# Storing the last tile of a rotary embedding in two pieces of four rows

## Chip, cores and metric

One core of a Trainium2 chip. The metric is the device time of one execution in microseconds (us).

In the text and the profiles, PE is the matmul engine (TensorE), DVE is VectorE, ACT ScalarE, POOL GpSimd, SPq the sync engine's queue, which issues the transfers, and L83 is line 83 of the kernel. A transfer has landed when its last bytes are written. Each transfer here is carried by 16 DMA engines in packets; the packet records give each packet's start, duration and size, but not its engine, so packets were chained end to start to follow one engine.

## The reference

```python
batch, seq, dim, num_heads = 16, 512, 1024, 16       # head_dim 64, half 32, float32
x = x.reshape(batch, seq, num_heads, head_dim)
x1, x2 = x[..., :half], x[..., half:]
out = concatenate([x1*cos - x2*sin, x1*sin + x2*cos], axis=-1)
```

32 MiB come in, 32 MiB go out, and each element gets two products and a sum.

## The kernel before

The batch is worked in 8 tiles of 128 partitions x 8192 floats: a partition holds 8 rows ("rows" 0 to 7) of 1024 floats, so a tile is 4 MiB and one partition's share a contiguous 32 KB in HBM. Five tiles fit on chip (three buffers of 1, 2 and 2 tiles), and each is worked in place. All loads and stores but one small table go out from the sync engine's queue, in program order.

```python
def store(t):
    nc.sync.dma_start(out=out_v[t], in_=tiles[t])
def store_two(t):
    nc.sync.dma_start(out=out_v[t : t + 2].rearrange("t p f -> p t f"), in_=both(t))
...
def stores(t):
    if t == 4:
        store_two(3)
    elif t != 3:
        store(t)
    if t == 2:
        load(5)
        load_two(6)
...
for t in range(NT):                              # NT = 8
    ...                                          # row 0: DVE, PE, then ACT copies it back
    pair_sum(*p1, b1)                            # rows 1, 2 on DVE
    ...
    pair_sum(*p2, b2)                            # rows 4, 5 on DVE
    pe_half(ROW_PE, *h1)                         # row 3: second half, ACT copies it back
    p1 = pair_product(t, third[0])
    ...
    pair_sum(*p1, b1)                            # rows 6, 7: the tile's last DVE instruction
    stores(t)
```

GpSimd makes the sine products (but for row 0, where DVE does), DVE the cosine products and most sums. Rows 0 and 3 are summed on PE and copied back by ACT.

Of the kernel before, what the change touches and what calls it, by code (L numbers as in the profile page):

```python
# [26 lines left out]
def kernel(  # L27
# [13 lines left out]
    nc = tc.nc  # L41
    P = nc.NUM_PARTITIONS
    batch, seq, dim = x.shape
# [4 lines left out]
    KK = seq // PB  # L48
    NT = batch // NB
# [3 lines left out]
    out_v = out.rearrange("(t b) (p k) h d -> t (b p) (k h d)", b=NB, k=KK)  # L53
# [14 lines left out]
    tiles = [places[t % len(places)] for t in range(NT)]  # L68
    first_of = [sum(HOMES[:i]) for i in range(len(HOMES))]

    def both(t):

        return homes[first_of.index(t % len(places))]

    def load(t, lo=0, hi=KK):
        s = slice(lo * dim, hi * dim)
        nc.sync.dma_start(out=tiles[t][:, s], in_=x_v[t][:, s])

    def load_two(t):
        nc.sync.dma_start(out=both(t), in_=x_v[t : t + 2].rearrange("t p f -> p t f"))  # L80

    def store(t):
        nc.sync.dma_start(out=out_v[t], in_=tiles[t])  # L83

    def store_two(t):
        nc.sync.dma_start(out=out_v[t : t + 2].rearrange("t p f -> p t f"), in_=both(t))
# [21 lines left out]
    for ps in (own_ps[:, :BANK], own_ps[:, BANK:], pe_ps):  # L108
# [9 lines left out]
        out=spread.rearrange("p (b q) -> p b q", b=NB),  # L118
        in_=bass.AP(tensor=eye.tensor, offset=eye.offset, ap=[eye.ap[0], [0, NB], [1, PB]]),
# [79 lines left out]
    def stores(t):  # L199
        if t == 4:  # L200
            store_two(3)
        elif t != 3:
            store(t)
        if t == 2:
            load(5)
            load_two(6)

    cos_product(own_ps, rows(0, ROW_OWN), ROW_OWN)
    for t in range(NT):
        first, second, third = PAIRS  # L210
        b1 = sin_rows(t, first[0], 2)
        p1 = pair_product(t, first[0])
        r0 = rows(t, ROW_OWN)
        own_product(r0)
        for ps, r in zip(parts(own_ps), parts(r0)):
            pe_add(ps, swapped(r))
        nc.scalar.copy(out=r0, in_=own_ps)  # L217
        b3 = sin_rows(t, ROW_PE, 1)
        b2 = sin_rows(t, second[0], 2)
        pair_sum(*p1, b1)  # L220
        h0, h1 = zip(parts(rows(t, ROW_PE)), parts(b3))
        pe_half(ROW_PE, *h0)
        p2 = pair_product(t, second[0])
        b1 = sin_rows(t, third[0], 2)
        pair_sum(*p2, b2)
        pe_half(ROW_PE, *h1)
        p1 = pair_product(t, third[0])
        if t + 1 < NT:
            cos_product(own_ps, rows(t + 1, ROW_OWN), ROW_OWN)
        pair_sum(*p1, b1)  # L230
        stores(t)
# [35 lines left out]
```

## Time and profile before

| | before |
|---|---|
| median of the first 3 runs | 162.31 us (162.19 to 162.6) |
| span of the profiled execution | 160.6 us |
| DVE, GpSimd, PE, ACT busy | 85%, 79%, 35%, 11% |
| main DMA queue, share of 16 engines' span | 97.8% |
| bytes moved, mean rate over the span | 67.25 MB, 419 GB/s |

The span runs from the first instruction to the last; the time also has what lies around it, about 1.7 us. "16 engines" are those that move the data of every transfer.

### The profile page before, as it was taken

The page shows a single profiled execution, that of the slowest core. Times are in us where ns is not written, and L with a number is a line of the kernel's source. Part 1 is how long each engine was busy: PE and PEld are TensorE (multiplying, and loading weights), DVE is VectorE, ACT ScalarE, POOL GpSimd, SP SyncE. Part 2 cuts the span into 40 slices and gives each one's busy share as a digit, 9 for nine tenths or more (in the row PEclk, how much of TensorE's full clock was granted, in tenths as well). Part 3 has the DMA queues.
Part 4 walks back from the last instruction along what each step waited for, and adds up shares of the span by engine and source line. Part 5 has one row for each costly group of instructions (what it writes and reads, how often), then busy time and mean ns, then how long its engine had stood idle before and what let it go on. Part 6 is the DMA issues. An engine that isn't in the chain of part 4 may idle for free.

```text
span 160.6 us, 431 instructions
## 1 busy us (share of the span) xinstructions
PE 56.2 (35%) x71; PEld 18.8 (12%) x71; DVE 136.4 (85%) x85; ACT 18.1 (11%) x25; POOL 127.1 (79%) x38
## 2 busy tenths in 40 slices
PE   3043905073505550282209140835055502822000
PEld 0021201030102110121003000301021101210000
DVE  1079979999999999999999999999999999998000
ACT  0003301003100301030101210031003010301000
POOL 1059999999999999988998799982999999960000
PEclk9999985559555855576556855595558555765555
DMA  5999999999999999999999999999999999999993
GB/s 187 401 408 473 392 490 424 392 433 482 392 392 522 392 392 522 392 392 498 410 400 465 441 400 408 498 392 408 498 400 400 506 400 400 473 433 400 433 465 147
DMA packets 2561, 67.25 MB, mean 419 GB/s; under 512 B 256, under 2 KB 384, under 8 KB 384
## 3 DMA queue, kind: packets, MB, share of 16 engines
q1 hardware_dynamic: 2480, 67.18, 97.8%
q10 hardware_dynamic: 80, 0.07, 0.1%
q14 instruction: 1, 0.01, 0.0%
HBM read 33.69 MB, written 33.55 MB: 419 GB/s over the span
## 4 chain that ended last, share of the span: by engine, by line
DVE 43%; DMA 34%; issue 7%; POOL 7%; PE 1%; DVEq 0%; SPq 0%
DVE x L197 21%; DVE pd L149 18%; DMA x<-in_x_dram 18%; DMA out_dram<-x 12%; POOL b L173 7%; DMA b<-in_sin_dram 4%; DVE pe_ps L149 2%; PE pd L121 1%; DVE sns L124 0%; DVE sns L125 0%; DVE own_ps L149 0%; DVE x L158 0%; DVEq L197 0%; SPq L80 0%; SPq L83 0%
## 5 line engine op out<-in xcount | busy, mean ns | idle before, releaser
L173 POOL TENSOR_TENSOR b<-x,sns 128x2048 f32<-128x2048 f32 (+1 forms) x32 | 126.4, 3989 | 15.4 <-DVE sns L125 8.6
L197 DVE TENSOR_TENSOR x<-pd,b 128x2048 f32<-128x2048 f32 x24 | 54.9, 2287 | 2.3 <-POOL b L173 1.5
L149 DVE TENSOR_TENSOR pd<-x,tab 128x2048 f32<-128x2048 f32 x24 | 55.0, 2292 | 0.2
L184 PE MATMUL own_ps<-x,ident 128*128 128x512 f32 x32 | 28.9, 1059 | 53.6 <-DVE x L158 48.6
L184 PE MATMUL pe_ps<-b,ident 128*128 128x512 f32 x32 | 25.2, 880 | 29.2 <-DVE pe_ps L149 29.2
L184 PEld LDWEIGHTS own_ps<-x,ident 128*128 128x128 f32 x32 | 9.4, 324 | 73.6 <-DVE x L158 59.6
L217 ACT COPY x<-own_ps 128x1024 f32<-128x1024 f32 x8 | 8.1, 1012 | 72.3 <-PE own_ps L184 72.3
L189 ACT COPY x<-pe_ps 128x512 f32<-128x512 f32 x16 | 9.4, 588 | 40.8 <-PE pe_ps L184 40.8
L184 PEld LDWEIGHTS pe_ps<-b,ident 128*128 128x128 f32 x32 | 8.0, 280 | 43.7 <-DVE pe_ps L149 36.1
L149 DVE TENSOR_TENSOR pe_ps<-x,tab 128x512 f32<-128x512 f32 x16 | 11.0, 686 | 0.0
L149 DVE TENSOR_TENSOR own_ps<-x,tab 128x1024 f32<-128x1024 f32 x8 | 9.8, 1224 | 0.3 <-DMA x<-in_x_dram 0.2
L158 DVE TENSOR_TENSOR x<-x,tab 128x1024 f32<-128x1024 f32 x8 | 9.7, 1214 | 0.0
L124 DVE TENSOR_SCALAR sns<-pd 128x256 f32<-128x256 f32 x1 | 0.4, 425 | 7.5 <-PE pd L121 7.5
L121 PE MATMUL pd<-b,spread 64*128 64x256 f32 x2 | 1.2, 697 | 5.2 <-DMA b<-in_sin_dram 5.2
L217 ACT ACT_TABLE_LOAD x1 | 1.3, 1283 | 14.8 <-DVE x L158 14.8
L109 PE MATMUL own_ps<-zero 128*128 128x512 bf16 x2 | 1.0, 621 | 1.2 <-DVE zero L105 1.2
L121 PEld LDWEIGHTS pd<-b,spread 64*128 64x128 f32 x2 | 0.5, 310 | 6.1 <-issue 6.1
L122 PE MATMUL tab<-b,spread 64*128 64x256 f32 x2 | 1.1, 631 | 0.0
L105 DVE MEMSET zero<- 128x256 uint32 x1 | 0.3, 272 | 0.9 <-PEq L248 0.9
L122 PEld LDWEIGHTS tab<-b,spread 64*128 64x128 f32 x2 | 0.7, 334 | 0.2
L109 PE MATMUL pe_ps<-zero 128*128 128x512 bf16 x1 | 0.6, 634 | 0.0
L109 PEld LDWEIGHTS <-zero 128*128 128x128 bf16 x3 | 0.3, 124 | 1.5 <-DVE zero L105 1.2
(9 smaller groups left out, 1.8 us busy)
## 6 DMA issues: line engine op xcount, KB each, us to landing
out_dram<-x SPq DMA_DIRECT2D x6, 4096.0 KB, 21.9
x<-in_x_dram SPq DMA_DIRECT2D x2, 8192.0 KB, 39.1
x<-in_x_dram SPq DMA_DIRECT2D x3, 4096.0 KB, 27.7
out_dram<-x SPq DMA_DIRECT2D x1, 8192.0 KB, 33.1
x<-in_x_dram SPq DMA_DIRECT2D x1, 2560.0 KB, 12.0
x<-in_x_dram SPq DMA_DIRECT2D x1, 1536.0 KB, 6.8
b<-in_sin_dram ACTq DMA_DIRECT2D x1, 64.0 KB, 7.0
b<-in_cos_dram SPq DMA_DIRECT2D x1, 64.0 KB, 6.7
```

Of the source, the lines that this page charges most:

```text
L105: nc.vector.memset(zero, 0.0)
L109: nc.tensor.matmul(out=ps, lhsT=zero[:, :P], rhs=zero, start=True, stop=True)
L121: nc.tensor.matmul(out=sin_t, lhsT=spread, rhs=sin_sb, start=True, stop=True)
L122: nc.tensor.matmul(out=cos_t, lhsT=spread, rhs=cos_sb, start=True, stop=True)
L124: nc.vector.tensor_scalar_mul(out=sns[:, :, 0, :], in0=sin_k, scalar1=-1.0)
L149: nc.vector.tensor_tensor(out=o, in0=i, in1=cb, op=ALU.mult)
L158: nc.vector.tensor_tensor(out=heads(r), in0=heads(r), in1=s, op=ALU.mult)
L173: nc.gpsimd.tensor_tensor(out=o, in0=i, in1=sb, op=ALU.mult)
L184: nc.tensor.matmul(out=ps, lhsT=ident, rhs=other, start=False, stop=True, skip_group_check=True)
L189: nc.scalar.copy(out=r, in_=pe_ps)
L197: nc.vector.tensor_tensor(out=r, in0=ps, in1=b, op=ALU.add)
L217: nc.scalar.copy(out=r0, in_=own_ps)
```

## The change

It means to shorten the tail: rows 0 to 3 of the last tile are finished before rows 6 and 7, so their half of the store can be issued before the last DVE sum.

```diff
-    def store(t):
-        nc.sync.dma_start(out=out_v[t], in_=tiles[t])
+    def store(t, lo=0, hi=KK):
+        s = slice(lo * dim, hi * dim)
+        nc.sync.dma_start(out=out_v[t][:, s], in_=tiles[t][:, s])
...
         if t == 4:
             store_two(3)
+        elif t == NT - 1:
+            store(t, 0, KK // 2)
+            store(t, KK // 2)
         elif t != 3:
             store(t)
```

## The prediction

> **What bounds the kernel now.** I started with the page's busy totals, its slices and its table of DMA queues, because they disagree about the bound. DVE is busy 85% of the span and the chain that ended last gives DVE 43%, but the DMA queues show hardly any slack:
>
> ```profile
> PE 56.2 (35%) x71; PEld 18.8 (12%) x71; DVE 136.4 (85%) x85; ACT 18.1 (11%) x25; POOL 127.1 (79%) x38
> ...
> DVE  1079979999999999999999999999999999998000
> ...
> DMA  5999999999999999999999999999999999999993
> ...
> q1 hardware_dynamic: 2480, 67.18, 97.8%
> ...
> DVE 43%; DMA 34%; issue 7%; POOL 7%; PE 1%; DVEq 0%; SPq 0%
> ```
>
> The packets of queue q1 take 97.8% of 16 engines' span of 160.6 us, that is 157.0 us on each engine. The DMA row stands at 9 in every slice but the first and the last, while DVE has nothing to do in the last three slices (some 12 us). A DMA share of 34% in the chain means only that the chain is followed back through DVE where a store waited for a sum; it doesn't mean that the queue was ever empty. So the end is set by bytes: 67.18 MB through 16 engines. Outside those 157.0 us lie about 1.7 us until the first data moves, about 1.2 us after the last packet, and some 0.6 us of anything else.
>
> Then I looked at the end, which is all that the change touches. The timeline of the last instructions, and the DMA queue's own waits from 100 us on:
>
> ```profile
> 145.46 0.59 ACT L189 COPY x<-pe_ps 128x512 f32<-128x512 f32 x1 [4.92 <-PE pe_ps L184]
> 145.60 2.29 DVE L197 TENSOR_TENSOR x<-pd,b 128x2048 f32<-128x2048 f32 x1
> ...
> 147.96 0.33 SPq L83 DMA_DIRECT2D out_dram<-x  x1
> ...
> SPq L83 <- DVE x L197: 49.0, 3, 16.8
> SPq L262 <- DMA out_dram<-x: 11.2, 2, 9.6
> ```
>
> The last ACT copy (second half of row 3) ends at 146.05, the last DVE sum (rows 6 and 7) at 147.89; the last store is issued at 147.96, and the final wait on the landings (L262) takes another 9.6 us at the longest. The obvious reading is that a store of 4 MB stands exposed after the last sum and that starting half of it early shortens the tail. Whether that holds depends on what the 16 engines do at 148 us. So I asked for the DMA share in stretches of 0.25 us (columns: stretch, its length, busy time of the engines, clock, DMA share, GB/s):
>
> ```profile
> 147.50:147.75 0.25, 0.00 (x0) 0.00 (x0) 0.25 (x1) 0.00 (x0) 0.00 (x0) 0.50 2.73 1180
> 147.75:148.00 0.25, 0.00 (x0) 0.00 (x0) 0.14 (x1) 0.00 (x0) 0.00 (x0) 0.50 1.21 524
> 148.00:148.25 0.25, 0.00 (x0) 0.00 (x0) 0.00 (x0) 0.00 (x0) 0.00 (x0) 0.50 0.31 131
> 148.25:148.50 0.25, 0.00 (x0) 0.00 (x0) 0.00 (x0) 0.00 (x0) 0.00 (x0) 0.50 0.00 0
> 148.50:148.75 0.25, 0.00 (x0) 0.00 (x0) 0.00 (x0) 0.00 (x0) 0.00 (x0) 0.50 0.31 131
> 148.75:149.00 0.25, 0.00 (x0) 0.00 (x0) 0.00 (x0) 0.00 (x0) 0.00 (x0) 0.50 3.98 1704
> 149.00:149.25 0.25, 0.00 (x0) 0.00 (x0) 0.00 (x0) 0.00 (x0) 0.00 (x0) 0.50 0.31 131
> ...
> 150.00:150.25 0.25, 0.00 (x0) 0.00 (x0) 0.00 (x0) 0.00 (x0) 0.00 (x0) 0.50 4.33 1835
> ...
> 158.00:158.25 0.25, 0.00 (x0) 0.00 (x0) 0.00 (x0) 0.00 (x0) 0.00 (x0) 0.50 0.30 131
> ```
>
> A packet is counted whole where it starts, so the shares come in bursts. One packet of 32 KB adds 131 GB/s to such a stretch, and a share of 0.303: 0.303 x 0.25 us x 16 engines = 1.21 us for one packet (the packet records give a median of 1213 ns over 1920 packets). The burst at 147.50 to 148.00 is (1180 + 524) / 131 = 13 packets, the next is 13 at 148.75 to 149.00, the next 14 at 150.00 to 150.25: the engines start a new packet about every 1.22 us, straight across the point where the store of tile 6 ends and the store of tile 7 begins (about 148.8). In the packet records, the engine that comes last ends its share of tile 6 at 149.72 and starts its share of tile 7 at 149.72; the one with the longest gap there waits 0.15 us and isn't the last. So the last store comes just in time, about 0.85 us after its issue began, to a queue that has just drained. The engine that comes last starts its final packet at 158.19 and ends it at 159.40.
>
> **What the Trainium skill says.** Page "DMA: Bandwidth & Descriptors", section "Queues, rings and completion order": on each engine descriptors are consumed in ring order. The trace agrees: no engine shows tile 7's packets ahead of tile 6's. A piece issued earlier from the same queue therefore waits behind tile 6.
>
> Same page, section "Rules for kernel authors": two transfers to disjoint partition halves aren't worth it, since they "share the same engines either way". This change cuts along the rows, not the partitions, but the reason carries over: each piece still has 128 partitions, and all 16 engines carry it.
>
> Same page, "Anatomy of one DMA": a fixed cost of about 2.0 us (measured there for another issuing path), mostly completion. Here one trails only after the very last packet: that ends at 159.40, and the final wait passes at 159.75, so 0.35 us; between stores none is seen.
>
> **The change part by part.** The listing of instruction order in the built changed program shows PE, DVE, ACT and POOL unchanged, line numbers aside. On the DMA queue the store of 128x8192 becomes two of 128x4096: the first waits for ACT alone, the second for DVE alone.
>
> 1. First piece: ready when the last ACT copy is done (146.05 instead of 147.89), so issued about 1.85 us earlier. Its packets still queue behind tile 6, until about 148.8 on most engines and 149.72 on the last. Gain on the last engine: 0. Gain on the others: the gap of up to 0.15 us, which doesn't set the end.
>
> 2. Second piece: issued at about 147.96 as now, while the first moves. The first lasts 2.10 MB at 16 x 32768 B / 1.213 us = 432 GB/s, so 4.85 us, to about 153.7. The second's packets, there from about 148.8, have 4.9 us to spare. No gap between the two.
>
> 3. Packet size: each engine moves 16 packets of 16 KB where it moved 8 of 32 KB. The first tile's load has the other sizes: in the packet records 12 KB takes 460 ns and 20 KB 766 ns (medians). Halfway, 16 KB is 613 ns (my estimate), so 16 x 613 = 9808 ns against 8 x 1213 = 9704 ns: **+0.10 us**.
>
> 4. One more transfer: a completion packet of 4 B (9 ns in the records) on each engine, and one wait more among the last ones, which will have passed long before the end. At most +0.02 us.
>
> Sum for the end: 0 + 0 + 0.10 + 0.02 = +0.12 us, so 162.31 + 0.12 = 162.4 us. All else, the loads and the DVE sums that gate them, lies before 144 us and is untouched.
>
> **The rivals.** (a) The tail is exposed, and half of it moves ahead. If the engines had been idle before 148.8, the first piece would start 1.85 us sooner and, with the second behind it without a gap, the end would come 1.85 us sooner: 160.5, or 1.1% less. For it speaks the 9.6 us wait at L262; against it the bursts, which leave no idle time to start in. Even this rival doesn't reach 2%, since no piece can start before 146.05. A weaker form is possible: the store comes only just in time, and in unprofiled executions the gap could be a few tenths larger, which the split would close. That would give 162.0 to 162.2.
>
> (b) Packets of 16 KB cut out of rows of 32 KB write slower. The tiles' stores move whole rows; no write of this size is in the trace. Only the first tile's loads use part rows, and they lose about 1%. If writes lost 10%, the tail would grow by 1.0 us, to 163.3; 2% of the time would need a third more on these 9.7 us. I give that one chance in a hundred.
>
> (c) The seventeenth transfer waits for an earlier one, because the semaphores of the DMAs are used in turn (16 transfers on 8 of them before). The listing shows no such wait: the second piece waits for DVE alone. If one came up, it could only be for a transfer landed long ago.
>
> **Range and chances.** The three runs of before span 162.19 to 162.6, and that spread is larger than my +0.12. Below I leave room for the weak form of (a), above for a mild (b): 161.9 to 162.9. Faster by over 2% would need 159.1, beyond what rival (a) gives; slower by over 2% would need 165.6.
>
> **What would show it.** Right: the first piece's issue at about 146.1, the second at 148.0; bursts of packets that go on across 148.8 without a stretch of 1 us lacking any; packets of 16 KB at about 613 ns; the last packet's end at 159.4 to 159.6 and a span of 160.6 to 160.8. Step 1 is wrong if tile 7's packets start before 148.6, step 3 if a 16 KB packet takes much other than 0.61 us. The prediction fails if the first piece moves beside tile 6 and the two together run above 432 GB/s, or if 16 KB writes are far slower than 16 KB reads.

## More of the kernel before

The prediction shows the lines that bound the kernel. To them belong the page's DMA issues, from issue to landing:

```profile
out_dram<-x SPq DMA_DIRECT2D x6, 4096.0 KB, 21.9
...
out_dram<-x SPq DMA_DIRECT2D x1, 8192.0 KB, 33.1
```

A store of 4 MB takes some 10 us of the 16 engines but lands 21.9 us after its issue (median): it waits behind others. And in the ten us after the last store's packets start (stretch, length, busy times, clock, DMA share, GB/s) no compute engine has work, while the DMA engines are full:

```profile
148.70:158.70 10.00, 0.00 (x0) 0.00 (x0) 0.00 (x0) 0.00 (x0) 0.00 (x0) 0.50 0.98 419
```

## The result, and the profile after

| | before | after |
|---|---|---|
| median of 6 runs each | 162.28 us (162.19 to 162.6) | 162.45 us (162.23 to 162.64) |
| ratio after / before | | 1.0008, 95% interval 0.9995 to 1.0021 |
| span of the profiled execution | 160.6 us | 160.4 us |

A ratio is the mean time of one kernel's runs over that of the other's of the same rounds, so it isn't quite the ratio of the medians. The two times are the same within noise. The page of the changed kernel, for DVE, the DMA engines and the main queue:

```profile
DVE  1079879999999999999999999999999999998000
...
DMA  5999999999999999999999999999999999999994
...
q1 hardware_dynamic: 2624, 67.18, 97.9%
```

The same picture, with 144 packets more: 128 from cutting the last tile's 128 packets of 32 KB into 256 of 16 KB, and 16 for one more transfer's completion. The timeline of the end and the DMA queue's waits from 100 us on:

```profile
145.29 0.59 ACT L190 COPY x<-pe_ps 128x512 f32<-128x512 f32 x1 [4.88 <-PE pe_ps L185]
145.43 2.29 DVE L198 TENSOR_TENSOR x<-pd,b 128x2048 f32<-128x2048 f32 x1
145.90 2.17 SPq L84 DMA_DIRECT2D out_dram<-x  x2
...
SPq L84 <- ACT x L190: 13.8, 1, 13.8
SPq L266 <- DMA out_dram<-x: 11.3, 1, 11.3
```

The first piece waited for the ACT copy and went out at 145.90, while the last sum ran; the second followed at 147.75 (the line merges both: 145.90 + 2.17 = 148.07 is the end of the second's issue). So the half store was issued 1.85 us before the other, as the change intends. But the final wait on the landings is as long as it was: 11.3 us in one piece, where the kernel before had 11.2 us in two (L262 in the prediction's lines: 1.6 us for tile 6, then 9.6 us for tile 7). The DMA share in stretches of 0.25 us, in which a packet is counted whole where it starts, shows why:

```profile
148.00:148.25 0.25, 0.00 (x0) 0.00 (x0) 0.00 (x0) 0.00 (x0) 0.00 (x0) 0.50 0.61 262
148.25:148.50 0.25, 0.00 (x0) 0.00 (x0) 0.00 (x0) 0.00 (x0) 0.00 (x0) 0.50 0.00 0
148.50:148.75 0.25, 0.00 (x0) 0.00 (x0) 0.00 (x0) 0.00 (x0) 0.00 (x0) 0.50 1.08 459
148.75:149.00 0.25, 0.00 (x0) 0.00 (x0) 0.00 (x0) 0.00 (x0) 0.00 (x0) 0.50 0.78 328
149.00:149.25 0.25, 0.00 (x0) 0.00 (x0) 0.00 (x0) 0.00 (x0) 0.00 (x0) 0.50 0.92 393
...
158.50:158.75 0.25, 0.00 (x0) 0.00 (x0) 0.00 (x0) 0.00 (x0) 0.00 (x0) 0.50 0.17 66
```

From 148.56 on the bursts are finer, because the packets are half as long; no packet of 16 KB starts before that, 2.66 us after its issue. The first piece simply waited in the queue: in the packet records each engine starts its first packet of 16 KB within a few ns after its last one of tile 6. The ten us that answer to those of before:

```profile
148.50:158.50 10.00, 0.00 (x0) 0.00 (x0) 0.00 (x0) 0.00 (x0) 0.00 (x0) 0.50 0.98 418
```

### The profile page after: what moved, and what is told of

It is laid out like the page before. It is cut to its first block, busy times and chain, and to the rows that moved or that the text cites. A ratio compares the mean times of both kernels' runs of the same rounds, so it can differ in the third digit from the quotient of the medians.

```text
span 160.4 us, 431 instructions
## 1 busy us (share of the span) xinstructions
PE 56.4 (35%) x71; PEld 18.8 (12%) x71; DVE 136.4 (85%) x85; ACT 18.1 (11%) x25; POOL 127.0 (79%) x38
## 4 chain that ended last, share of the span: by engine, by line
DVE 43%; DMA 34%; issue 7%; POOL 7%; PE 1%; DVEq 0%; SPq 0%
DVE x L198 21%; DVE pd L150 18%; DMA x<-in_x_dram 18%; DMA out_dram<-x 12%; POOL b L174 7%; DMA b<-in_sin_dram 4%; DVE pe_ps L150 2%; PE pd L122 1%; DVE sns L125 0%; DVE sns L126 0%; DVE own_ps L150 0%; DVE x L159 0%; DVEq L198 0%; SPq L80 0%; DVEq L150 0%
```

## The experiments

Theory: the 16 engines have no idle time before the last store, so earliness is worth nothing, and smaller packets cost a few hundredths of a us. Main rival (A): the tail is exposed, the earlier issue does gain up to 1.8 us, and the split costs as much elsewhere. All kernels were right but the one marked. The next three and "all stores in halves" ran in the same rounds (before: 162.32 us, 11 runs), the four with delays in others (before: 162.32, 7 runs).

**The change once more.** No edit.

> The changed kernel unaltered, as the measure for the others of these rounds. My theory (the engines are still moving tile 6 until 148.8 us, so the earlier issue gains nothing, and packets of 16 KB at 611 ns cost 16 x 611 - 8 x 1213 = 72 ns more): +0.05 to +0.15 us against before, about 162.4. Rival A (the earlier issue gains up to 1.8 us, and smaller packets or the extra transfer cost as much): the same time, so it is the next two runs that tell the two apart.

Measured: 162.59 us (162.22 to 163.18), ratio 1.0016 (0.9994 to 1.0039). The same as before within noise; the medians differ by 0.27 us, more than the 0.05 to 0.15 expected, but the spread is larger than the effect sought.

**The split without its earliness.**

```diff
-            store(t, 0, KK // 2)
-            store(t, KK // 2)
+            store(t, KK // 2)
+            store(t, 0, KK // 2)
```

> The same two pieces, but rows 4 to 7 are stored first: both pieces now wait for the last DVE sum, so that the earliness is gone and the packet size and the number of transfers stay. My theory: first piece issued at about 147.9 us, time within 0.15 us of the changed kernel. Rival A: the gain of up to 1.8 us is lost and the cost stays, so 163.3 to 164.2. Rival B (a small gap at the hand-over is closed by the split): 0.1 to 0.3 us slower than the changed kernel.

Measured: 162.41 us (162.35 to 162.73), ratio 1.0004 (0.9989 to 1.0018). The timeline of the sync queue's last issues in this run:

```profile
147.90 0.81 SPq L84 DMA_DIRECT2D out_dram<-x  x2
```

Both pieces now go out after the last sum, and nothing is lost. Rival A, which had 163.3 or more, falls. The time is 0.18 us under the changed kernel's in these rounds, where at most 0.15 either way was expected; the spreads cover that. Rival B, which had it slower, isn't seen.

**Earliness without the split** (result wrong).

```diff
-        pair_sum(*p1, b1)
+        if t < NT - 1:
+            pair_sum(*p1, b1)
```

> Wrong on purpose: the whole store, but without the last DVE sum, so that rows 6 and 7 of the last tile are stored as they were loaded and the last store can go at about 146.1 us instead of 147.96, with no smaller packets. My theory: the store waits behind tile 6, time 0 to 0.15 us under before. Rival A (the tail after the last sum is exposed): 1.8 us less, 160.5.

Measured: 162.28 us (162.24 to 162.69), ratio 1.0001 (0.9985 to 1.0017). The sync queue's last issue:

```profile
145.44 0.33 SPq L83 DMA_DIRECT2D out_dram<-x  x1
```

The whole store is out 2.5 us earlier than in the kernel before, DVE does one instruction less, and the time is the same. The kernel isn't bound by its last sum. (The store went out 0.66 us earlier than the expected 146.1 us, because the ACT copy was done sooner; the argument doesn't rest on that.)

**A late last sum, with the whole and with the split store.** DVE repeats the last product, once or four times, ahead of the last sum; each is tried on the kernel before ("whole") and on the changed one ("split"). They were run on another chip.

```diff
+        if t == NT - 1:
+            for _ in range(1):                   # or 4
+                cos_product(*p1, third[0], 2)
         pair_sum(*p1, b1)
         stores(t)
```

> The kernel before with the product of rows 6 and 7 of the last tile done once more on DVE ahead of the last sum (same result): the last store is ready 2.2 to 2.3 us later, at about 150.2 us. My theory: the store of tile 6 ends at 148.8 on most engines and 149.7 on the last, and the new store's packets come only at about 151.1, so the queue runs empty: +1.4 to +2.3 us, 163.7 to 164.6. Rival E (the queue holds more work than I read, so a late store costs nothing): +0 to +0.3.

> The changed kernel with the same extra product. My theory: the first piece is issued at 146.1 us as ever and keeps the engines busy to about 153.7, the second comes at about 151.1: no gap, time within 0.2 us of the changed kernel, about 162.4, so 1.3 to 2.2 us faster than the whole store with the same delay. Rival E: no difference from the whole store.

> The kernel before with four extra products, 4 x 2.2 to 2.3 = 9.0 us of delay. My theory: the engines stand idle from about 149 to 157.8 us, +8.1 to +9.1 us, 170.4 to 171.4.

> The changed kernel with four extra products. My theory: the first piece runs from 148.8 to 153.7 us inside the delay, the second starts at about 157.8 and takes 8 x 611 ns = 4.9 us: +3.2 to +4.2 us against before, 165.5 to 166.5, so some 4.9 us faster than the whole store with the same delay. That is all that the split can ever gain. Rival A (the two pieces gain by their number, whatever the queue does): a difference nearer to 1.8 us, as with no delay.

| extra products | whole | split | whole - split |
|---|---|---|---|
| 0 (the rounds of the first result) | 162.28 | 162.45 | -0.2 |
| 1 | 164.01 (ratio to before 1.0099) | 162.32 (1.0005) | 1.7 |
| 4 | 170.91 (1.0527) | 166.28 (1.0244) | 4.6 |

All four lie where they were expected. Rival E, by which a late store costs nothing or the split gains nothing, falls: with one extra product the whole store is slower than before by 1.0% (0.8 to 1.2), the split store isn't.

The DMA share in stretches chosen around the hand-over, one extra product. Whole store:

```profile
148.50:151.25 2.75, 0.00 (x0) 0.00 (x0) 1.95 (x1) 0.00 (x0) 0.00 (x0) 0.50 0.03 12
151.25:161.25 10.00, 0.00 (x0) 0.00 (x0) 0.00 (x0) 0.00 (x0) 0.00 (x0) 0.50 0.98 419
```

Split store:

```profile
148.50:151.25 2.75, 0.00 (x0) 0.00 (x0) 2.15 (x1) 0.00 (x0) 0.00 (x0) 0.50 0.95 405
```

With the whole store the engines stand idle while DVE ends its sum; the share falls from 0.98 to 0.03. With the split store the first piece fills the same stretch at 405 GB/s. So the change's mechanism works, as soon as there is idle time for it. With four extra products, whole and then split:

```profile
148.50:154.00 5.50, 0.00 (x0) 0.00 (x0) 5.43 (x3) 0.00 (x0) 0.00 (x0) 0.50 0.00 0
154.00:157.90 3.90, 0.00 (x0) 0.00 (x0) 2.95 (x2) 0.00 (x0) 0.00 (x0) 0.50 0.00 0
```

```profile
148.50:154.00 5.50, 0.00 (x0) 0.00 (x0) 5.43 (x3) 0.00 (x0) 0.00 (x0) 0.50 0.90 384
154.00:158.00 4.00, 0.00 (x0) 0.00 (x0) 3.21 (x2) 0.00 (x0) 0.00 (x0) 0.50 0.01 4
```

The first piece runs inside the delay and then the engines wait for the second. The gain of 4.6 us is close to the 4.9 us that one piece takes (8 packets of 611 ns on each engine); in these two profiles the split's last sum also ended 0.25 us later (157.31 against 157.06), which makes up the rest. So the duration of one piece is the ceiling of this split.

One extra product delayed the whole store's issue by 2.56 us (150.52 against 147.96) but the time by only 1.7. In the kernel before, one engine trailed the others by some 0.7 us; the idle time lets it catch up (last engine's end 161.26 against a mean of 161.16). The mean end thus moved by 2.46 us and the last one by 1.86, so that part of the delay is hidden. This is read from two profiles, not tested.

**What smaller packets cost.** All stores in halves, or the last tile in single rows; both with the later rows first, so that nothing goes out early.

```diff
-        if t == 4:
-            store_two(3)
...
+        n = KK // 2
+        for lo in reversed(range(0, KK, n)):
+            if t == 4:
+                store_two(3, lo, lo + n)
+            elif t != 3:
+                store(t, lo, lo + n)
```

> All stores cut into two pieces of four rows, the later rows first so that nothing is issued earlier: 23 transfers. It multiplies the packet cost by eight. My theory: 256 KB more per engine in 16 KB packets for each tile, 8 tiles x 72 ns = 0.58 us, less what overlaps elsewhere: +0.4 to +0.8 us against before, about 162.9. Rival C (16 KB packets beside loads cost more than alone, or the reused semaphores make the stores wait): over +1.5 us. Rival D (no cost at all): within 0.15 us of before.

Measured: 162.75 us (162.6 to 163.12), ratio 1.0025 (1.0009 to 1.0040), so +0.4 us (0.0025 x 162.3).

```diff
-            store(t, 0, KK // 2)
-            store(t, KK // 2)
+            for k in reversed(range(KK)):
+                store(t, k, k + 1)
```

> The last tile in eight pieces of one row each, last row first, so that nothing is issued earlier: packets of 4 KB. From 1213 ns at 32 KB and 611 at 16 KB a packet costs 9 ns beyond its bytes, so 4 KB should take about 160 ns and the last tile 64 x 160 = 10.2 us instead of 9.7 on each engine. Theory (the cost goes by packets): +0.4 to +0.6 us against before, 162.7 to 162.9. Rival F (it goes by transfers, some 0.07 us for each one added, whatever the packets): +0.5 as well here, but then the run by partitions, with as many transfers, is as slow. Rival G (no cost that shows): within 0.15 us.

Measured: 162.63 us (162.49 to 163.04), ratio 1.0021 (1.0007 to 1.0036), so +0.34 us, somewhat under what was expected. (Before in these rounds: 162.29, 8 runs, for this and the next. They were run on another chip.) The packet records fit: 16 KB took 611 ns and 4 KB 159 ns (medians). Packet time per engine, summed over the main queue, was 157.08 us before, 157.66 with all stores in halves (+0.58, which is 8 x 72 ns) and 157.77 with single rows (+0.69); the other runs with whole stores of all 128 partitions range from 156.95 to 157.08. Both are slower than before with the interval clear of 1, by a quarter of a per cent: storing in smaller pieces does cost. That the packets cost it is read from the records; by time alone these two runs don't tell packets from transfers (each adds seven transfers). The next run was to do that.

**As many transfers, but whole rows.** The last tile in 8 transfers of 16 partitions.

```diff
-            store(t, 0, KK // 2)
-            store(t, KK // 2)
+            for i in range(8):
+                nc.sync.dma_start(out=out_v[t][i::8], in_=tiles[t][i::8])
```

> The last tile in eight transfers too, but of 16 partitions each (every eighth one), whole rows of 32 KB: as many transfers as by single rows, and packets as large as before. Theory (the cost goes by packets): within 0.2 us of before. Rival F (it goes by transfers): +0.5 us, as by single rows. If partitions taken so load the engines unevenly it is slower still, which the packet records would show.

Measured: 172.31 us, ratio 1.0612 (1.0598 to 1.0627). Neither theory had 10 us; only the reserve at the end of the expectation allowed for it, and by uneven engines, which isn't what came. The last tile's packets of 32 KB took 2.5 us (median 2512 ns) where they took 1.2. The Trainium skill, page "SBUF — State Buffer", section "Door 1: The DMA port swizzle", says that a transfer's bandwidth goes by how many of 16 SBUF ports its partitions reach, and its table puts every eighth partition on 8 of the 16. Two more kernels tested that: two transfers of 64 partitions, neighbouring (8 ports by that table), or every second one (16 ports).

```diff
+            for h in (slice(0, P // 2), slice(P // 2, P)):      # or slice(0, P, 2), slice(1, P, 2)
+                nc.sync.dma_start(out=out_v[t][h], in_=tiles[t][h])
```

> The last tile in two transfers of 64 neighbouring partitions each (0 to 63, then 64 to 127), whole rows of 32 KB. The run by every eighth partition took 10 us more, its packets 2.5 us instead of 1.2. Theory P (what halves the rate is the set of partitions of one transfer: the Trainium skill's page on SBUF gives 8 of 16 ports to partitions 0 to 63): packets of some 2.4 us and 8 to 10 us over before here too. Rival Q (it was the many small transfers of 16 partitions): here, with two transfers, within 0.3 us of before.

> The last tile in two transfers of 64 partitions each, the even ones, then the odd ones, whole rows of 32 KB. Every second partition reaches all 16 ports by that page's table. Theory P: near to before, 0 to 2 us over it, depending on whether the engines hit different ports at the same moment; packets of 1.2 us where they do. Rival R (any transfer of fewer than 128 partitions, or with a partition step, runs at half the rate): 8 to 10 us over before, as for neighbouring halves.

Measured (before: 162.31, 6 runs): neighbouring halves 172.15 us, ratio 1.0604 (1.0585 to 1.0623); every second partition 162.73 us (162.21 to 163.18), ratio 1.0012 (0.9982 to 1.0042). They were run on another chip. The last store's stretch, neighbouring halves first:

```profile
149.00:169.00 20.00, 0.00 (x0) 0.00 (x0) 0.00 (x0) 0.00 (x0) 0.00 (x0) 0.50 0.98 210
```

```profile
149.60:159.60 10.00, 0.00 (x0) 0.00 (x0) 0.00 (x0) 0.00 (x0) 0.00 (x0) 0.50 0.98 419
```

The engines are as busy in both, at half the rate in the first. Two transfers alone aren't the cause, nor is a partition step, nor fewer than 128 partitions: rivals Q and R fall, and the times are as the page's table says. These cuts also change which HBM rows are written together, and no run holds that fixed; but neighbouring halves (2 MB in one piece of HBM) and every eighth partition (rows 256 KB apart) differ most in that and were equally slow. The run by every eighth partition thus could not tell transfers from packets, and every second partition adds just one transfer; what a transfer alone costs stays open beyond its completion packet of 9 ns.

No version beat both kernels. None was to be expected from an earlier store at the end of the program: what runs there is a queue that is full already.

## Why the prediction was right

- **No idle time at the hand-over (step 1): right.** Shown from both sides: earliness without the split, and the split without earliness, changed nothing; idle time made on purpose brought the gain at once. Rival (a) fell. By the letter its sign of being wrong came up (tile 7's packets started at 148.56 us, before 148.6), but behind tile 6, on an execution that ran about 0.17 us ahead. The 9.6 us that the prediction reads as the final wait's length are its second part alone; the whole wait took 11.2.
- **The second piece comes in time (step 2): right.** It was issued at 147.75, and no stretch between 148.5 and 158.5 lacks packets.
- **Packet size (step 3): right in kind, its +0.10 us too large for this pair of profiles.** 16 KB took 611 ns, not 613. And the 32 KB packets of the kernel before took 1218 ns on average in the last store, not the median of 1213 that the sum used. So per engine it is 16 x 611 = 9776 against 8 x 1218.4 = 9747 ns: +0.03 us. An early issue seems to hide the rest: packets issued early took 1213 (no last sum) or 611 exactly, those issued just in time 1218 or, split late, 615.7 ns on average. Like with like, smaller packets so cost 16 x 611 - 8 x 1213 = 72 ns when early and 16 x 615.7 - 8 x 1218.4 = 104 ns when just in time, which is step 3's size; the change goes from the one kind to the other. That is a pattern of a few profiles, not a tested cause.
- **One more transfer (step 4):** the completion packet of 9 ns is there; a cost beyond it was not resolved.
- **The sum.** +0.12 us was predicted and +0.17 measured between the medians, but the interval reaches from -0.08 to +0.34 us (ratios 0.9995 and 1.0021). "No difference that these runs can show" is what stands; the sign isn't shown, and that 0.12 lies so near to 0.17 is luck. The profile's last packet ended at 159.19, not within 159.4 to 159.6, and the span was 160.4, not 160.6 or more: that execution's last DVE sum ended 0.17 us earlier as well (147.72 against 147.89), so all of it ran ahead by about as much.
- **The rivals.** The weak form of (a), a gap at the hand-over that the split closes, is there, but too small: in the kernel before, up to 3 of the 16 engines stood without a packet between 148.67 and 149.00 us, the last one to end not among them; in the changed kernel at most one did, for some 10 ns at a time. The 0.1 to 0.3 us that it was to gain lie outside the interval. (b) and (c) didn't come: 16 KB writes took 611 ns, where the estimate from the reads was 613, and no wait for an earlier transfer appears among the queue's waits.

## What to carry to other kernels

Before you cut a last store to start it early, ask whether the DMA engines are idle between the moment when the early piece could be issued and the moment when the whole store is; a long final wait on the landings doesn't say so, but the DMA share in short stretches does. If they are busy, the early piece only queues; if they are idle, the gain is at most the smaller of the idle time and the piece's own duration. And cut along the free axis, or by partitions that still reach all ports: halves by neighbouring partitions cost 10 us on a 4 MB store here.

## What the Trainium skill lacked or had wrong

- "DMA: Bandwidth & Descriptors", "Rules for kernel authors", says not to bother with two transfers of partition halves since both use the same engines. The rule names no cost, and here there is one: neighbouring halves took 172.15 us against 162.31, every second partition 162.73. The page "SBUF — State Buffer" has what is missing, in its port table, and its rate for 8 ports (an asymptote of some 218 GB/s) agrees with the 210 measured; the rule doesn't point there.
- "DMA: Bandwidth & Descriptors", "Where 436 GB/s comes from", says that for HBM to SBUF and back the HBM side of about 358 GB/s binds. Put so, it doesn't hold for one core at work: these runs moved 419 GB/s over a whole span of loads and stores, and also in a stretch of stores alone. The skill isn't without this (its own measured table for one core reaches 425); it is this sentence that lacks the condition.
- "DMA: Bandwidth & Descriptors", "Anatomy of one DMA", gives about 2.0 us of fixed cost, most of it completion, for the other issuing path; for the sync queue the page has a first-byte latency (some 600 ns) but no completion. Here the first packet came 0.83 us after the issue began and 0.50 us after it ended, to idle engines (150.52 to 151.35 with the whole store and one extra product), and the last wait passed 0.35 us after the last packet (0.42 in the changed kernel).
- No page says how far the 16 engines drift apart under a full queue: in the kernel before the last engine ended at 159.40 against a mean of 158.70, without the last sum 1.1 us after the mean; after a stretch of idleness 0.1 us. A transfer lands with its slowest engine, so this drift is of the size of the effects sought here.
